# One whole-chunk subtraction on VectorE for the lower parts of U and V in a PEER kernel

## The chip, the cores and the metric

The kernel runs on one core of a Trainium2 chip. The metric is the device time of one execution in microseconds. The core has five engines with queues of their own, each of which runs its instructions in order: TensorE (PE in the profile, with its weight loads as PEld), VectorE (DVE), ScalarE (ACT), GpSimd (POOL) and SyncE (SP, which here only issues loads). Semaphores set the order between them.

## The reference, cut to what matters

Two layers run over 256 latent and 256 context tokens of width 1024: a gMLP mixer, then a state-space mixer, each followed by a PEER expert block. Of the context, only layer 0's result is needed. The change concerns the PEER blocks, whose 16384 experts (128 x 128 keys) each own a row of `u_tab` and of `v_tab`:

```python
q = (hb @ w_q).reshape(PEER_BLOCK, PEER_HEADS, 2, PEER_DHALF)
s = jnp.einsum("nhkd,hkmd->nhkm", q, sub_keys)
s_half, i_half = lax.top_k(s, PEER_TOPK)
...
ids = k1 * PEER_KEYS + k2
g = jax.nn.softmax(top_s, axis=-1)
ue = jnp.take(u_tab, ids, axis=0)
ve = jnp.take(v_tab, ids, axis=0)
act = jax.nn.gelu(jnp.einsum("nd,nhkd->nhk", hb, ue))
return jnp.einsum("nhk,nhkd->nd", g * act, ve)
```

## The kernel before

The kernel doesn't gather experts for most tokens. It computes every expert's activation for a block of tokens as a dense product, multiplies it with a matrix of gates that is zero where an expert wasn't chosen, and multiplies the result with the whole of V. In layer 0 this dense stage takes 384 tokens (`n`), and the remaining 128 context tokens go by gathered rows, with GpSimd issuing the indirect loads and VectorE doing the dot products (tile `gscr`, L611) and the weighted sums (tile `acc`, L624). In layer 1 all 256 tokens go through the dense stage.

The 16384 experts are taken in 128 chunks of 128. `front(k1)` (L707) loads a chunk of U (tile `ur`, 128 x 1024, 512 KB), multiplies it with the tokens and applies the gelu (`act`); `back(k1)` (L726) loads a chunk of V (`vr`), multiplies the activations with the gates (`w`, L741) and adds the product with V to sums that stay in PSUM.

Each float32 matrix product is made of three matmuls on a reduced-precision type: every operand is split into an upper part and a lower part (upper times upper, upper times lower, lower times upper; `mm3`, L305, for U, and L755 to L757 for V). `split` (L297) makes the upper part on ScalarE, a copy with a rounding (tiles `uh`, `vh`, `wh`), and the lower part by subtracting it from the source (`ul`, `vl`, `wl`, L303), on VectorE or on GpSimd: a counter `turn` and the two last arguments give the shares of the two.

Before the change each chunk of U and of V is split in two halves of 512 columns. U's halves go by `DV0 = (1, 2)` in layer 0 (one in three on VectorE) and by (1, 1) in layer 1; V's halves go by (1, 1). `UB = 5` halves of U and `VB = 4` halves of V are held. The raw chunks have buffers of their own: 3 for U (`UR`), 2 for V in layer 0 and 4 in layer 1 (`VR`).

The order of the work in `dense` (L692): first 62 chunks of U in layer 0 and 66 in layer 1 (`ahead` less 2), together with the routing and the making of the gates (`during`: VectorE makes `eq` and `o`, L676 and L680, TensorE multiplies them, L664 and L665). Results that aren't kept are written to memory. Then the loop over all 128 chunks of V runs, where for the remaining chunks `front(k1 + 8)` stands ahead of `back(k1)`. So the V loop begins with chunks of V alone and goes on with U and V in turn. In layer 0 the gathers are spread over this loop (`pump`). In the V loop TensorE's order is the program's; on the other engines a planner places each instruction by a simulated time. In layer 1's first stretch U's splits have a higher priority (`HP = (0, 1000)`).

Of the kernel before, what the change touches and what calls it, by code (L numbers as in the profile page):

```python
# [10 lines left out]
F32R = mybir.dt.float32r  # L11
# [7 lines left out]
P = 128  # L19
D = 1024  # L20
KB = D // P
# [4 lines left out]
KEYS = 128  # L26
# [20 lines left out]
TAIL0 = 0  # L47
WB = 2
KEEP0 = 8
UB = 5  # L50
VB = 4
ROWS = 4
EARLY0 = 8
MID0 = 18
AHEAD1 = 68
TAIL1 = 0
M = SEQ // L
HP = (0, 1000)
# [5 lines left out]
AR_ = (2, 4)  # L64
UR = (3, 3)
ACTB = (1, 2)
DV1 = (1, 1)
DV0 = (1, 2)
DVS = (DV0, (1, 1))
VV0 = (1, 1)  # L70
VV1 = (1, 1)
F1 = 4
PIN = 1
HA = 50
# [37 lines left out]
def tile_hybrid(ctx: ExitStack, tc: tile.TileContext, I, out, stop=None):  # L112
    nc = tc.nc
# [19 lines left out]
    def load(dst, src):  # L133
        return nc.sync.dma_start(dst, src)  # L134
# [162 lines left out]
    def split(hi, lo, src, dve=1, gps=1):  # L297


        turn[0] += 1  # L300
        nc.scalar.activation(hi, src, AF.Copy)  # L301
        e = nc.vector if turn[0] % (dve + gps) < dve else nc.gpsimd
        return e.tensor_tensor(lo, src, hi.bitcast(F32), op=OP.subtract)  # L303
# [386 lines left out]
    act_d = dr.tile([KEYS, P, NDENSE], F32, name="act_d")  # L690

    def dense(pd, back_pool, i, n, hh, hl, ahead, keep, abanks, vbanks, during, between, pump,  # L692
              dve=(0, 1), vdve=(1, 1), finish=None):


        nb = (n + P - 1) // P
        acts, gts = {}, {}
        kg, ng = 8, n // GT

        def gate_rows(blk, g0, g1):  # L700

            if blk not in gts:
                gts[blk] = pb.tile([P, ng, kg, GT], F32, name="Gr")
            load(gts[blk][:, g0:g1].rearrange("p g k n -> p g (k n)"),
                 gd[i][g0:g1, :, blk * kg:(blk + 1) * kg, :].rearrange("g p k n -> p g (k n)"))

        def front(k1, spill=False):  # L707
            u = pd.tile([P, KB, KEYS], F32, name="ur", bufs=UR[i])
            load(u, I[f"peer_ut{i}"][k1])
            pairs = []  # L710
            for q in range(2):
                uh = pd.tile([P, KB // 2, KEYS], F32R, name="uh", bufs=UB)
                ul = pd.tile([P, KB // 2, KEYS], F32R, name="ul", bufs=UB)
                with tc.high_priority(HP[i]) if k1 < ahead and HP[i] else ExitStack():
                    split(uh, ul, u[:, q * 4:q * 4 + 4], *(dve if k1 < ahead else DVS[i]))
                pairs += [((uh[:, b], ul[:, b]), (hh[:, 4 * q + b], hl[:, 4 * q + b])) for b in range(4)]
            pm = ps.tile([P, 512], F32, name=f"bk{abanks[k1 % len(abanks)]}")
            mm3(pm[:, :n], pairs)
            act = pd.tile([P, n], F32, name="act", bufs=keep + ACTB[i])
            nc.scalar.activation(act, pm[:, :n], AF.Gelu_apprx_tanh)  # L720
            if spill:
                eng[QS[2]].dma_start(act_d[k1, :, 0:n], act)
            else:
                acts[k1] = act

        def back(k1):  # L726
            blk, j = divmod(k1, kg)
            v = pb.tile([P, D], F32, name="vr", bufs=VR[i])
            load(v, I[f"peer_v{i}"][k1 * KEYS:(k1 + 1) * KEYS, :])
            if k1 in acts:  # L730
                act = acts.pop(k1)
            else:
                act = pb.tile([P, n], F32, name="actr", bufs=AR_[i])
                load(act, act_d[k1, :, 0:n])
            if k1 == 0:
                for g0 in range(0, ng, GB):
                    gate_rows(0, g0, min(ng, g0 + GB))
            if (blk + 1) * kg < KEYS:
                gate_rows(blk + 1, ng * j // kg, ng * (j + 1) // kg)
            w = pb.tile([P, n], F32, name="w", bufs=WB)  # L740
            nc.vector.tensor_tensor(w.rearrange("p (g n) -> p g n", n=GT),  # L741
                                    act.rearrange("p (g n) -> p g n", n=GT),
                                    gts[blk][:, :, j, :], op=OP.mult)
            wh = pb.tile([P, n], F32R, name="wh", bufs=WB + 1)
            wl = pb.tile([P, n], F32R, name="wl", bufs=WB + 1)
            ends["w"] = split(wh, wl, w, 1, 0).ins
            first, last = k1 == 0, k1 == KEYS - 1
            for q in range(2):
                vh = pb.tile([P, 512], F32R, name="vh", bufs=VB)
                vl = pb.tile([P, 512], F32R, name="vl", bufs=VB)  # L750
                split(vh, vl, v[:, q * 512:(q + 1) * 512], *vdve)
                for t in range(nb):
                    js = slice(t * P, min(n, (t + 1) * P))
                    o = vacc[t][q][0:js.stop - js.start]
                    nc.tensor.matmul(o, wh[:, js], vh, start=first, stop=False)  # L755
                    nc.tensor.matmul(o, wh[:, js], vl, start=False, stop=False)  # L756
                    nc.tensor.matmul(o, wl[:, js], vh, start=False, stop=last)  # L757

        for k1 in range(ahead - TF[i]):
            front(k1, k1 < ahead - keep)  # L760
            during(k1)
        between()
        with tc.issue_after(ends["gates"]):
            for k1 in range(ahead - TF[i], ahead):
                front(k1)
        order = tc.manual_schedule(engines={mybir.EngineType.PE})
        order.__enter__()
        pb = back_pool()
        vacc = [[ps.tile([P, 512], F32, name=f"bk{vbanks[2 * j + q]}") for q in range(2)] for j in range(nb)]
        total = 2 * KEYS - ahead  # L770
        done = 0
        for k1 in range(KEYS):
            if ahead <= k1 + keep < KEYS:
                front(k1 + keep)
                done += 1
            back(k1)
            done += 1
            pump(done / total)
        order.__exit__(None, None, None)
        if finish:  # L780
            return finish(vacc)
        use_banks(*abanks)
        for j in range(nb):
            m = min(n - j * P, P)
            acc = pb.tile([P, D], F32, name="vr", bufs=VR[i])
            for q in range(2):
                nc.scalar.copy(acc[0:m, q * 512:(q + 1) * 512], vacc[j][q][0:m])
            with urgent(HD):
                add_back(i, acc, j * P, m)
# [462 lines left out]
    def layer0():  # L1252
        n = NDENSE
# [52 lines left out]
        with pool("hx") as ph, pool("hold", side="right") as pk, ExitStack() as hold:  # L1306
            hh = ph.tile([P, KB, n], F32R, name="hxh")
            hl = ph.tile([P, KB, n], F32R, name="hxl")
# [10 lines left out]
            with pool("hc") as pc:  # L1319
# [4 lines left out]
                ahead = [next(weights)]  # L1324
# [39 lines left out]
            with pool("de0", 2) as pd, ExitStack() as rs:  # L1364
                early = EARLY0
                first = spread((work, 250, 0, 1), (gathers, early, 0, 1))
                rest = []

                def during(k):
                    first((k + 1) / (AHEAD0 - TAIL0 - TF[0]))  # L1370

                def between():
                    drain(work)
                    scr.close()
                    pa = rs.enter_context(pool("ada1", 2, side="right"))
                    cB = ada_silu(pa) if CB else None
                    phases = phase_units(pa)
                    ada = ada_rows(pa, LATE[NS:NQ], cB)
                    cut = (AHEAD0 - KEEP0) / (2 * KEYS - AHEAD0)
                    rest.append(spread((gathers, MID0, 0.0, cut), (gathers, 128 - early - MID0, cut, GEND), (phases, 53, *PW),  # L1380
                                       (ada, NQ - NS, *AW)))
                    use_banks(1)
                    rs.callback(lambda: [drain(gathers), drain(ada), drain(phases)])

                def back_work(t):
                    with tc.issue_after(ends["w"]) if PB_ <= t < PC_ else ExitStack():
                        rest[0](t)

                use_banks(2, 3, 4, 5, 6, 7)
                dense(pd, lambda: rs.enter_context(pool("db0", 2, side="right")), 0, n, hh, hl, AHEAD0, KEEP0, (0, 1), (2, 3, 4, 5, 6, 7),  # L1390
                      during, between, back_work, DV0, VV0)
            use_banks(*range(8))

    def layer1():
        n = SEQ
# [19 lines left out]
        with pool("hx1") as ph:  # L1415
            hh = ph.tile([P, KB, n], F32R, name="hxh")
            hl = ph.tile([P, KB, n], F32R, name="hxl")
# [7 lines left out]
            with pool("sc1", 2, side="right") as pw:  # L1425
                weights = score_weights(1, pw)
                ahead = [next(weights)]
# [8 lines left out]
            with pool("de1", 2) as pd, ExitStack() as rs:  # L1436
# [55 lines left out]
                        rest[0](t)  # L1492

                use_banks(2, 3, 4, 5, 6, 7)
                dense(pd, lambda: pd, 1, n, hh, hl, AHEAD1, 8, (0, 1), (4, 5, 6, 7), during, between, back_work1, DV1, VV1, finish)
                use_banks(*range(8))

    layer0()
# [66 lines left out]
```

## Time and profile before

| | us |
|---|---|
| median of 3 runs | 3009.76 (3003.44 to 3010.11) |
| the profiled execution | 2998.49 |
| its span | 2996.7 |
| TensorE busy | 2678.1 (89%) |
| VectorE busy | 2306.5 (77%) |
| ScalarE busy | 1307.0 (44%) |
| GpSimd busy | 1438.1 (48%) |

Shares over the whole span hide that the stretches differ. In the trace the dense stage of layer 0 lies from about 480 to 1830 us and that of layer 1 from about 2130 us to the end; between them, and before, other code runs that the change doesn't touch. A busy time is the time between an instruction's start and its end, whatever it did in it. "Idle before" is the time in which the engine had no instruction running just before one of a group, with what released it. In the names, `bk` is a PSUM bank, and `out<-in` tells what an instruction writes and reads.

### The profile page before, as it was taken

The numbers are of one execution on the slowest core, as the hardware profiler recorded it, in microseconds if no ns is written. First come the engines' busy times: TensorE is split into PE (matmuls) and PEld (weight loads), VectorE is DVE, ScalarE is ACT, GpSimd is POOL, SyncE is SP. The second block draws the span as 40 slices with busy tenths as digits, with TensorE's granted clock in tenths as the row PEclk, the third lists the DMA queues.
The fourth block names the chain that finished last, engine by engine and source line by source line (L and its number), as shares of the span: only waits on it lengthen the run. The fifth ranks groups of instructions, "written<-read, shape, count | busy, mean of one in ns | idle before, by whom it ended". The sixth has DMA issues, their size and how long they took to land.

```text
span 2996.7 us, 46002 instructions
## 1 busy us (share of the span) xinstructions
PE 2678.1 (89%) x16231; PEld 2375.2 (79%) x16231; DVE 2306.5 (77%) x3980; ACT 1307.0 (44%) x2412; POOL 1438.1 (48%) x1008
## 2 busy tenths in 40 slices
PE   6799899888878888999999987998788889999998
PEld 2599798888766666888888866798787888899997
DVE  7796879999977886999999986464899876644344
ACT  4553243354562233333333323334345665555554
POOL 2031134544634344788888871235454335544443
PEclk8899999999988999999999998999899999999999
DMA  8579743565658787898999987997366778866662
GB/s 276 156 241 338 258 152 123 179 223 191 228 201 268 266 295 255 310 319 311 326 305 316 312 271 253 332 342 204 113 197 232 284 266 297 275 213 216 204 208 104
DMA packets 414576, 738.89 MB, mean 247 GB/s; under 512 B 41604, under 2 KB 272260, under 8 KB 409224
## 3 DMA queue, kind: packets, MB, share of 16 engines
q1 hardware_dynamic: 310240, 507.84, 51.1%
q0 software_dynamic: 36864, 134.23, 13.1%
q10 hardware_dynamic: 67240, 93.88, 8.8%
q8 instruction: 127, 2.08, 0.3%
q14 instruction: 105, 0.86, 0.1%
HBM read 633.07 MB, written 102.77 MB: 246 GB/s over the span
## 4 chain that ended last, share of the span: by engine, by line
PE 31%; DMA 13%; DVE 11%; issue 7%; POOL 5%; ACT 1%; SPq 1%; DVEq 0%; ACTq 0%; POOLq 0%
PE bk L756 6%; PE bk L757 5%; PE bk L755 5%; PE bk L311 4%; PE bk L309 4%; PE bk L310 4%; DMA vr<-peer_v 3%; DMA row<-peer_v,ids 2%; POOL row L601 2%; DMA row<-peer_u,ids 2%; DVE ul L303 1%; POOL ul L303 1%; POOL vl L303 1%; PE bk L554 1%; SPq L134 1%
## 5 line engine op out<-in xcount | busy, mean ns | idle before, releaser
L311 PE MATMUL bk<-hxh,ul 128*128 128x384 f32 (+1 forms) x2048 | 649.5, 318 | 47.7 <-DVE ul L303 28.5
L309 PE MATMUL bk<-hxh,uh 128*128 128x384 f32 (+1 forms) x2048 | 649.6, 317 | 11.7 <-ACT uh L301 6.9
L310 PE MATMUL bk<-hxl,uh 128*128 128x384 f32 (+1 forms) x2048 | 643.8, 314 | 0.0
L303 POOL TENSOR_TENSOR ul<-ur,uh 128x512 fp32r<-128x512 f32 x299 | 447.1, 1501 | 301.9 <-ACT uh L301 268.7
L303 POOL TENSOR_TENSOR vl<-vr,vh 128x512 fp32r<-128x512 f32 x256 | 363.0, 1422 | 461.1 <-ACT vh L301 454.6
L756 PE MATMUL bk<-vl,wh 128*128 128x512 f32 x1280 | 517.8, 405 | 63.6 <-POOL vl L303 46.1
L755 PE MATMUL bk<-vh,wh 128*128 128x512 f32 x1280 | 511.5, 400 | 36.8 <-ACT wh L301 19.5
L301 ACT ACTIVATE vh<-vr 128x512 fp32r<-128x512 f32 x512 | 315.4, 623 | 519.2 <-DMA vr<-peer_v 375.9
L757 PE MATMUL bk<-vh,wl 128*128 128x512 f32 x1280 | 509.0, 398 | 0.0
L301 ACT ACTIVATE uh<-ur 128x512 fp32r<-128x512 f32 x512 | 315.5, 629 | 408.4 <-PE bk L310 226.6
L311 PEld LDWEIGHTS bk<-hxh,ul 128*128 128x128 f32 x2048 | 397.5, 194 | 55.5 <-DVE ul L303 33.8
L309 PEld LDWEIGHTS bk<-hxh,uh 128*128 128x128 f32 x2048 | 398.3, 194 | 18.9 <-ACT uh L301 7.9
L310 PEld LDWEIGHTS bk<-hxl,uh 128*128 128x128 f32 x2048 | 398.2, 194 | 5.0
L303 DVE TENSOR_TENSOR wl<-w,wh 128x384 fp32r<-128x384 f32 (+1 forms) x256 | 192.6, 753 | 242.0 <-ACT wh L301 241.4
L756 PEld LDWEIGHTS bk<-vl,wh 128*128 128x128 f32 x1280 | 246.8, 193 | 135.3 <-POOL vl L303 62.4
L755 PEld LDWEIGHTS bk<-vh,wh 128*128 128x128 f32 x1280 | 246.5, 193 | 92.0 <-ACT vh L301 22.7
L757 PEld LDWEIGHTS bk<-vh,wl 128*128 128x128 f32 x1280 | 247.1, 193 | 50.7 <-DVE wl L303 0.3
L303 DVE TENSOR_TENSOR vl<-vr,vh 128x512 fp32r<-128x512 f32 x256 | 205.2, 812 | 74.4 <-ACT vh L301 73.5
L624 DVE SCALAR_TENSOR_TENSOR acc<-row,wts,acc 128x1024 f32<-128x1024 f32 x127 | 208.3, 1640 | 21.2 <-DMA row<-peer_v,ids 20.1
L611 DVE SCALAR_TENSOR_TENSOR gscr<-row,hn 128x1024 f16<-128x1024 f32 x128 | 209.7, 1639 | 18.3 <-DMA row<-peer_u,ids 17.1
L303 DVE TENSOR_TENSOR ul<-ur,uh 128x512 fp32r<-128x512 f32 x213 | 188.7, 888 | 43.5 <-ACT uh L301 41.7
L223 DVE SCALAR_TENSOR_TENSOR adasv<-adatv,cB 128x1024 f16<-128x1024 f32 x112 | 157.3, 1405 | 61.0 <-DMA adatv<-ada_t 60.1
(325 smaller groups left out, 4966.1 us busy)
## 6 DMA issues: line engine op xcount, KB each, us to landing
ur<-peer_ut SPq DMA_DIRECT2D x256, 512.0 KB
vr<-peer_v SPq DMA_DIRECT2D x256, 512.0 KB
gd<-Gs ACTq DMA_DIRECT2D x40, 1024.0 KB
adatv<-ada_t SPq DMA_DIRECT2D x72, 512.0 KB
wqT<-peer_w_q SPq DMA_DIRECT2D x64, 512.0 KB
Gr<-gd SPq DMA_DIRECT2D x120, 192.0 KB
wp<-wpo ACTq DMA_DIRECT2D x32, 512.0 KB
wpi<-wp SPq DMA_DIRECT2D x16, 1024.0 KB
```

Of the source, the lines that this page charges most:

```text
L223: e.scalar_tensor_tensor(scr, w, 1.0, cB[:, t], op0=OP.mult, op1=OP.mult, accum_out=mod[:, i, f, t:t + 1])
L301: nc.scalar.activation(hi, src, AF.Copy)
L303: return e.tensor_tensor(lo, src, hi.bitcast(F32), op=OP.subtract)
L309: nc.tensor.matmul(o, ah, bh, start=(i == 0), stop=False)
L310: nc.tensor.matmul(o, ah, bl, start=False, stop=False)
L311: last = nc.tensor.matmul(o, al, bh, start=False, stop=(i == n - 1))
L601: tc.keep_in_program_order(nc.gpsimd.indirect_dma_start(out=r[:], out_offset=None, in_=I[f"peer_{table}{i}"], in_offset=bass.IndirectOffse ...
L611: nc.vector.scalar_tensor_tensor(scr, r, 1.0, hn, op0=OP.mult, op1=OP.mult, accum_out=dots[:, h, k:k + 1])
L624: nc.vector.scalar_tensor_tensor(acc, r, w, acc, op0=OP.mult, op1=OP.add)
L755: nc.tensor.matmul(o, wh[:, js], vh, start=first, stop=False)
L756: nc.tensor.matmul(o, wh[:, js], vl, start=False, stop=False)
L757: nc.tensor.matmul(o, wl[:, js], vh, start=False, stop=last)
```

## The change

The two halves become one operation each: for every chunk ScalarE makes the upper part of all 1024 columns in one instruction, and VectorE makes the lower part of all 1024 columns in one instruction. GpSimd makes none of them. Two whole chunks of U and two of V are buffered. The shares and the arguments that passed them are gone. The matmuls are the same in number, shape and order. `turn`, which also deals out the subtractions of other splits in the kernel, counts fewer splits.

```diff
-UB = 5
-VB = 4
+UB = 2
+VB = 2
...
-DV1 = (1, 1)
-DV0 = (1, 2)
-DVS = (DV0, (1, 1))
-VV0 = (1, 1)
-VV1 = (1, 1)
...
         def front(k1, spill=False):
...
-            pairs = []
-            for q in range(2):
-                uh = pd.tile([P, KB // 2, KEYS], F32R, name="uh", bufs=UB)
-                ul = pd.tile([P, KB // 2, KEYS], F32R, name="ul", bufs=UB)
-                with tc.high_priority(HP[i]) if k1 < ahead and HP[i] else ExitStack():
-                    split(uh, ul, u[:, q * 4:q * 4 + 4], *(dve if k1 < ahead else DVS[i]))
-                pairs += [((uh[:, b], ul[:, b]), (hh[:, 4 * q + b], hl[:, 4 * q + b])) for b in range(4)]
+            uh = pd.tile([P, KB, KEYS], F32R, name="uh", bufs=UB)
+            ul = pd.tile([P, KB, KEYS], F32R, name="ul", bufs=UB)
+            with tc.high_priority(HP[i]) if k1 < ahead and HP[i] else ExitStack():
+                split(uh, ul, u, 1, 0)
+            pairs = [((uh[:, b], ul[:, b]), (hh[:, b], hl[:, b])) for b in range(KB)]
...
+            vh = pb.tile([P, D], F32R, name="vh", bufs=VB)
+            vl = pb.tile([P, D], F32R, name="vl", bufs=VB)
+            split(vh, vl, v, 1, 0)
             for q in range(2):
-                vh = pb.tile([P, 512], F32R, name="vh", bufs=VB)
-                vl = pb.tile([P, 512], F32R, name="vl", bufs=VB)
-                split(vh, vl, v[:, q * 512:(q + 1) * 512], *vdve)
+                qs = slice(q * 512, (q + 1) * 512)
                 for t in range(nb):
                     js = slice(t * P, min(n, (t + 1) * P))
                     o = vacc[t][q][0:js.stop - js.start]
-                    nc.tensor.matmul(o, wh[:, js], vh, start=first, stop=False)
-                    nc.tensor.matmul(o, wh[:, js], vl, start=False, stop=False)
-                    nc.tensor.matmul(o, wl[:, js], vh, start=False, stop=last)
+                    nc.tensor.matmul(o, wh[:, js], vh[:, qs], start=first, stop=False)
+                    nc.tensor.matmul(o, wh[:, js], vl[:, qs], start=False, stop=False)
+                    nc.tensor.matmul(o, wl[:, js], vh[:, qs], start=False, stop=last)
```

## Rows read from the trace of the kernel before

**Rows 1.** Busy time by stretch, all engines: stretch, length, PE, PEld, DVE, ACT, POOL, granted clock, DMA.

```profile
480.00:890.00 410.00, 349.52 (x2290) 331.04 (x2291) 396.80 (x951) 208.40 (x308) 205.40 (x134) 0.91 0.56 198
890.00:1200.00 310.00, 259.94 (x1025) 199.57 (x1023) 234.88 (x389) 94.51 (x178) 131.00 (x105) 0.94 0.81 271
1200.00:1745.00 545.00, 518.41 (x2595) 465.31 (x2595) 508.33 (x508) 191.72 (x377) 448.46 (x324) 1.00 0.91 313
...
2130.00:2470.00 340.00, 288.57 (x2418) 275.62 (x2418) 300.78 (x600) 191.51 (x327) 159.79 (x96) 0.94 0.68 235
2470.00:2620.00 150.00, 150.00 (x664) 124.20 (x663) 93.32 (x167) 86.86 (x166) 74.51 (x55) 1.00 0.87 285
2620.00:2997.00 377.00, 363.45 (x2293) 329.56 (x2291) 159.32 (x278) 199.67 (x389) 165.13 (x125) 0.99 0.57 189
```

**Rows 2.** Timeline of DVE from 1499 us: start, duration (us), engine, line, operation, form.

```profile
1499.61 0.55 DVE L303 TENSOR_TENSOR wl<-w,wh 128x384 fp32r<-128x384 f32 x1
1500.19 2.05 DVE L741 TENSOR_TENSOR w<-act,Gr 128x384 f32<-128x384 f32 x1
...
1505.51 1.22 DVE L611 SCALAR_TENSOR_TENSOR gscr<-row,hn 128x1024 f16<-128x1024 f32 x1
```

**Rows 3.** Timeline of POOL, same stretch.

```profile
1500.51 1.31 POOL L303 TENSOR_TENSOR vl<-vr,vh 128x512 fp32r<-128x512 f32 x1
1501.97 1.09 POOL L601 DMA_INDIRECT row<-peer_u,ids  x1 [0.16 <-issue]
...
1505.75 1.81 POOL L601 DMA_INDIRECT row<-peer_u,ids  x1 [1.37 <-DVE gscr L611]
```

**Rows 4.** Groups of DVE, 2470 to 2620 us: count, busy us and mean ns, idle before.

```profile
L303 DVE TENSOR_TENSOR vl<-vr,vh 128x512 fp32r<-128x512 f32 x56 | 36.1, 685 | 0.3 <-ACT vh L301 0.3
```

**Rows 5.** By tile (gscr, acc, o): ns minimum, median, maximum; first and last start, us.

```profile
L611 DVE SCALAR_TENSOR_TENSOR gscr<-row,hn x128: 1197/1221/4989, 532.6 to 1716.7; 128x1024 f16<-128x1024 f32 x128
L624 DVE SCALAR_TENSOR_TENSOR acc<-row,wts,acc x127: 1268/1284/3960, 1049.2 to 1801.5; 128x1024 f32<-128x1024 f32 x127
...
L680 DVE TENSOR_TENSOR o<-eq,gt x160: 662/683/2887, 613.3 to 2432.0; 128x1024 f16<-128x1024 f16 x160
```

**Rows 6.** Groups of DVE, 1200 to 1745 us.

```profile
L611 DVE SCALAR_TENSOR_TENSOR gscr<-row,hn 128x1024 f16<-128x1024 f32 x92 | 157.5, 1712 | 17.3 <-DMA row<-peer_u,ids 16.2
L624 DVE SCALAR_TENSOR_TENSOR acc<-row,wts,acc 128x1024 f32<-128x1024 f32 x89 | 150.0, 1686 | 12.4 <-DMA row<-peer_v,ids 11.4
L303 DVE TENSOR_TENSOR wl<-w,wh 128x384 fp32r<-128x384 f32 x62 | 65.7, 1060 | 6.1 <-ACT wh L301 6.1
L303 DVE TENSOR_TENSOR vl<-vr,vh 128x512 fp32r<-128x512 f32 x63 | 63.7, 1013 | 0.0
...
L303 DVE TENSOR_TENSOR ul<-ur,uh 128x512 fp32r<-128x512 f32 x40 | 36.8, 920 | 0.0
```

**Rows 7.** Waits of PE, 1200 to 1745 us: waiter <- releaser: total us, times, longest.

```profile
PE bk L756 <- POOL vl L303: 24.8, 20, 2.8
```

**Rows 8.** Groups of DVE, 480 to 890 us.

```profile
L680 DVE TENSOR_TENSOR o<-eq,gt 128x1024 f16<-128x1024 f16 x96 | 78.6, 864 | 0.1
...
L303 DVE TENSOR_TENSOR ul<-ur,uh 128x512 fp32r<-128x512 f32 x43 | 41.3, 960 | 1.7 <-ACT uh L301 1.7
```

**Rows 9.** Waits of PE, 480 to 890 us.

```profile
PE bk L664 <- DVE o L680: 31.4, 19, 4.7
```

**Rows 10.** Waits of PE, 2110 to 2470 us.

```profile
PE bk L311 <- POOL ul L303: 16.6, 5, 9.4
PE bk L311 <- DVE ul L303: 16.2, 11, 4.3
```

**Rows 11.** Waits of SP, the queue that issues loads, 890 to 1200 us.

```profile
SPq L134 <- DVE vl L303: 73.5, 35, 8.7
```

**Rows 12.** Groups of ACT, 2470 to 2620 us.

```profile
L301 ACT ACTIVATE vh<-vr 128x512 fp32r<-128x512 f32 x111 | 69.3, 624 | 37.9 <-PE bk L757 19.5 <-issue 17.4 <-DMA vr<-peer_v 1.1
```

**Rows 13.** Groups of POOL, 480 to 890 us.

```profile
L303 POOL TENSOR_TENSOR ul<-ur,uh 128x512 fp32r<-128x512 f32 x87 | 141.8, 1639 | 157.3 <-ACT uh L301 139.5 <-PE bk L310 7.8 <-DVE si L474 5.4
```

More of the change, by code (lines that the diff above doesn't have):

```diff
@@ L692, in dense @@
     def dense(pd, back_pool, i, n, hh, hl, ahead, keep, abanks, vbanks, during, between, pump,
-              dve=(0, 1), vdve=(1, 1), finish=None):
+              finish=None):
         nb = (n + P - 1) // P
@@ L1390, in layer0 @@
                 dense(pd, lambda: rs.enter_context(pool("db0", 2, side="right")), 0, n, hh, hl, AHEAD0, KEEP0, (0, 1), (2, 3, 4, 5, 6, 7),
-                      during, between, back_work, DV0, VV0)
+                      during, between, back_work)
             use_banks(*range(8))
@@ L1494, in layer1 @@
                 use_banks(2, 3, 4, 5, 6, 7)
-                dense(pd, lambda: pd, 1, n, hh, hl, AHEAD1, 8, (0, 1), (4, 5, 6, 7), during, between, back_work1, DV1, VV1, finish)
+                dense(pd, lambda: pd, 1, n, hh, hl, AHEAD1, 8, (0, 1), (4, 5, 6, 7), during, between, back_work1, finish)
                 use_banks(*range(8))
```

## Prediction, made before the changed kernel was run

> **What bounds the kernel now.** I read the profile in this order: the busy times by stretch, then in each stretch which wait TensorE suffers, then the durations of VectorE's operations against their shortest forms, then GpSimd's queue. The table by stretch [rows 1] shows six stretches that the change touches, with different limits. In the first, 480 to 890 us (62 chunks of layer 0's U, with routing and gate work), VectorE is busy 396.8 of 410 us: it sets the pace. From 890 to 1200 us (V alone, 56 chunks) no engine is full; TensorE has 259.9 of 310. From 1200 to 1745 us (U and V together, 62 chunks, with the row gathers) TensorE has 518.4 of 545, VectorE 508.3, GpSimd 448.5 and the DMA engines 0.91: everything is nearly full. From 2130 to 2470 us (layer 1's U) VectorE has 300.8 of 340 and TensorE 288.6. From 2470 to 2620 us (layer 1's V) TensorE has 150.00 of 150, and from 2620 to the end it is as full but for the finish. A gain must come from the first four stretches; the last two can only lose.
>
> The second thing to see is why VectorE is so full. At 1500.19 us the product w, 384 columns, takes 2.05 us, while the operation before it, with as many columns, takes 0.55 [rows 2]. GpSimd's subtraction began at 1500.51 us and took 1.31 [rows 3], so it ended at 1501.82, and w ended 0.42 us later: VectorE stood still inside its instruction until GpSimd's was over. That time is counted as busy. So VectorE's share overstates its work by what GpSimd's subtractions take from it.
>
> **The change part by part.** *The subtractions.* The 512 halves of U and 512 of V, shared by VectorE and GpSimd, all go; 256 operations of 1024 columns for U and 256 for V come, all on VectorE. An undisturbed half takes 0.685 us [rows 4]. No subtraction of 1024 columns is in this trace; the nearest row is the dot product gscr, two inputs of 1024 columns, 1.221 us at the median [rows 5]. It is bounded from below by one half, 0.685, and from above by two, 1.37. I take 1.22, since the columns are the same.
>
> *VectorE from 1200 to 1745 us.* Out go ul with 36.8 us and vl with 63.7 [rows 6]. In come 62 chunks times two operations times 1.22, 151 us. And the standing still goes: gscr takes 1.712 on average against 1.221, over 92 operations 45 us; acc 1.686 against 1.284, over 89, 36 us; wl 1.060 against the 0.55 of [rows 2], over 62, 32 us [rows 2, 5, 6]. All GpSimd subtractions of this stretch are ul and vl, so I let all of it go: 508.3 - 100.5 + 151 - 113 = 446 us. VectorE does the whole of the work that two engines shared and has less to do than now. GpSimd keeps only the row gathers. TensorE waits 24.8 us for GpSimd's vl here [rows 7], because in GpSimd's queue a subtraction stands behind gathers that wait for VectorE to free a row buffer. That queue is what the change removes; vl then stands behind gscr and acc on VectorE instead, each at most 1.28 us when nothing stops it. The ceiling is TensorE's 545 - 518 = 27 us; the DMA share puts a floor at 0.91 x 545 = 496 us, so transfers allow it but become tight. I take 18 us of gain, bounds 27 and 0.
>
> A page of the Trainium skill bears on this: "SBUF — State Buffer", section "Who interferes with whom", infers that a two-input VectorE operation does not hinder the writing of descriptors for GpSimd's own transfers, so the gathers would be free of VectorE. The trace speaks against it: a gather takes 1.09 us at 1501.97, and 1.81 at 1505.75, beside a gscr that had begun at 1505.51 [rows 2, 3]. By the page, VectorE's added subtractions cost GpSimd nothing; by the rows up to 0.7 us for each of some 180 gathers, 130 us, on a queue that gives up every subtraction of this stretch. Either way the sum stays.
>
> *The first stretch.* Out go 43 VectorE halves, 41.3 us; in come 62 times 1.22, 76 us. From o, 0.864 against its 0.683, come back 17 us over 96 operations [rows 5, 8]. What the other groups lose (397 less 41 and 79 for ul and o, so 277 us) I bound from both sides: nothing, or o's share, 0.181 of 0.864, 58 us. VectorE's total: 397 - 41 + 76 - 17 - (0 to 58) = 357 to 415 us. GpSimd keeps its few products of the routing, which go on stopping VectorE, and many of the groups are short scans, so I take 27 of the 58: 388, a gain of 9 at VectorE's present 97%. TensorE waits here for gate operands, 31.4 us [rows 9], and these come sooner if VectorE is less held. I take 10 us, bounds 40 and -20.
>
> *Layer 1's U, 2130 to 2470 us.* Here half of the subtractions are on VectorE already: some 68 halves go, at the first stretch's 0.960 [rows 8] 65 us, and 68 operations of 1.22 us come, 83 us; 64 gate products at o's 0.181 give back 12 and the other groups as much again at least. VectorE ends near 295 of 340, so it isn't the limit, and nothing is lost. TensorE's waits for ul, 16.6 and 16.2 us [rows 10], are the ceiling, 33 us. The single waits for GpSimd's ul are long (9.4 us at most), which is a queue, not a price. I take 10, bounds 33 and -20.
>
> *V alone in layer 0, 890 to 1200 us.* The V buffer vr has two slots, and SyncE's next load waits for the last vl of the chunk before last: 73.5 us on VectorE's alone [rows 11]. Now the chain from landing is two ScalarE halves and the later of two subtractions; then it is one ScalarE operation, at most two of 0.624 [rows 12], and one of 1.22. With the 1.31 of GpSimd's that is 1.25 + 1.31 now against 1.25 + 1.22 then: even. What VectorE no longer loses inside w and wl shortens its queue. I take 5, bounds 20 and -15. The last layer-0 chunks after 1745 us I put at 2.
>
> *Layer 1's V, TensorE full.* U keeps two chunks (two and a half before), V two (in halves before). TensorE's 664 matmuls in 150 us [rows 1] are 55 chunks of 2.71 us. A V buffer comes free when a chunk's last matmul is done; then ScalarE, at most two halves' 1.25 us [rows 12], VectorE 1.22, and 11 of 12 matmuls, 2.5 us, must pass before it is free again: at most 5.0 us in a loop that has two chunks, 5.42 us, to do it. It fits with some 0.4 us to spare, so I cost it at nothing; that cover is thin, and it is a rival. With U and V together the loop has a U chunk more and is safe.
>
> Sum: 18 + 10 + 10 + 5 + 2 = 45 us. The profiled execution took 2998.5 us (span 2996.7), 11 below the median of 3009.8; against itself it would become 2953, and the median 2965. **I forecast 2965 us**, own range 2920 to 2998.
>
> **The rivals.** *VectorE inherits GpSimd's wait (slower).* GpSimd's ul stood 139.5 us waiting for ScalarE's uh in the first stretch, over 87 operations 1.6 us each [rows 13], and it cost nothing since nothing urgent was behind it. On VectorE the gates, the products and the gathers' arithmetic are queued behind a subtraction that waits, and TensorE waits for those. If VectorE, less held, runs ahead of ScalarE and inherits half of that, 0.8 us on each of the 130 U chunks of the two front stretches, it is 104 us: 3009.8 - 45 + 104 = 3069. It turns the gain into a loss from 0.35 us a chunk on. Against: VectorE's own 43 halves waited only 1.7 us for uh there [rows 8]. Chance 0.14.
>
> *The gain is hidden anyway (no change).* VectorE's total in the first stretch stays near 397, inside its bounds, and from 1200 us the transfers at 0.91 set the pace in TensorE's place; what remains is 5 to 10 us from layer 1. That gives about 3003. For it speaks that a single short wait is easily replaced by the next. Chance 0.14.
>
> *Two V chunks are too few in layer 1.* If VectorE has both 256-column operations of the next chunk ahead of the one in the loop above (0.42 us each, by the step from 0.55 at 384 columns to 0.685 at 512 [rows 2, 4]), and ScalarE its split of w (under the 0.62 of 512 columns), the loop takes 6.4 us in place of 5.42, 0.5 us a chunk, over 55 chunks 27 us: 2992. Chance 0.12.
>
> That the change does not do what it says is excluded: with shares of 1 and 0 every such subtraction goes to VectorE.
>
> **How the numbers follow.** The forecast has 0.60. A measurement here tells about 0.3%, 9 us, from no change. Faster by more: 0.60 and most of the third rival, 0.70. Within it: the second rival, 0.14. Slower: the first rival and a little of the bounds, 0.16. The range reaches from 2915, where most of the four ceilings is reached (27 + 40 + 33 + 20 is 120, of which I allow 95), to 3025, where the first rival has begun; beyond it some 0.12 is left above and 0.06 below.
>
> **What would show it.** Right: gscr at 1.22 and acc at 1.28 on average from 1200 us on, ul and vl of 1024 columns near 1.22, 256 each, no ul or vl on GpSimd; TensorE's wait for vl there under 10 us and the stretch near 527; the V stretch of layer 1 still at 150 with TensorE full. Wrong: VectorE's ul with over 20 us of idle time before it, released by ScalarE's uh, in the first stretch; TensorE waiting for vl after 2470 us; or a V-only stretch of layer 0 that grows because vr is loaded later.

## The result and the profile after

| | us |
|---|---|
| before, median (4 runs) | 3009.94 (3003.44 to 3011.40) |
| after, median (4 runs) | 2900.35 (2896.73 to 2910.35) |
| ratio | 0.964, 95% interval 0.9617 to 0.9663 |
| after, the profiled execution | 2899.56, span 2897.8 |

The change takes 110 us, 3.6%, off the median. The direction was forecast; the size was more than twice the 45 us of the forecast, and the time lies below the range's lower end of 2915. The two profiled executions differ by 99 us, since that of before was 11 us below its median. What follows accounts for those 99.

To compare stretches whose ends move, each is cut at the same two instructions in every kernel: the first split of U, then the first, the 57th, the 121st and the last split of w in layer 0, the first split of U in layer 1, and the first, the 61st and the 121st split of w in layer 1. The table gives the time between their starts on ScalarE, in us.

| stretch | before | after | difference | forecast |
|---|---|---|---|---|
| layer 0, U with routing and gates | 421.0 | 419.1 | -2 | -10 |
| layer 0, V alone (56 chunks) | 287.9 | 269.8 | -18 | -5 |
| layer 0, U and V (64 chunks) | 559.4 | 520.8 | -39 | -18 |
| layer 0, last chunks | 56.1 | 43.4 | -13 | -2 |
| the mixer of layer 1, up to its U | 349.8 | 345.5 | -4 | 0 |
| layer 1, U with routing and gates | 299.0 | 275.0 | -24 | -10 |
| layer 1, V alone (60 chunks) | 160.0 | 160.6 | +1 | 0 |
| layer 1, U and V, and the finish | 381.4 | 381.4 | 0 | 0 |

Busy time by stretch, after (stretch, length, PE, PEld, DVE, ACT, POOL, granted clock, DMA share, GB/s), which answers [rows 1]:

```profile
480.00:900.00 420.00, 346.15 (x2313) 326.34 (x2313) 394.19 (x976) 198.29 (x246) 79.04 (x51) 0.91 0.59 204
900.00:1170.00 270.00, 237.31 (x967) 189.18 (x968) 207.15 (x382) 83.00 (x111) 43.19 (x45) 0.94 0.88 296
1170.00:1690.00 520.00, 519.38 (x2639) 473.69 (x2638) 442.83 (x549) 184.97 (x258) 254.75 (x191) 1.00 0.96 339
...
2060.00:2370.00 310.00, 276.51 (x2371) 265.87 (x2371) 281.12 (x579) 176.37 (x242) 30.60 (x16) 0.95 0.74 255
2370.00:2520.00 150.00, 150.00 (x663) 124.22 (x662) 114.57 (x166) 75.87 (x111) 0.00 (x0) 1.00 0.88 285
2520.00:2898.00 378.00, 364.53 (x2298) 330.43 (x2296) 219.73 (x281) 175.21 (x266) 0.00 (x0) 0.99 0.58 190
```

The third row is the one to see. TensorE is busy 519.38 of 520 us; VectorE, which now does all the subtractions, 442.83 (508.33 of 545 before); GpSimd 254.75 (448.46). In the first row VectorE still has 394 of 420.

Groups of DVE from 1170 to 1690 us, after (count, busy us and mean ns, idle before and its releasers), which answer [rows 6]:

```profile
L619 DVE SCALAR_TENSOR_TENSOR acc<-row,wts,acc 128x1024 f32<-128x1024 f32 x100 | 128.1, 1281 | 10.6 <-DMA row<-peer_v,ids 9.9
L606 DVE SCALAR_TENSOR_TENSOR gscr<-row,hn 128x1024 f16<-128x1024 f32 x92 | 112.2, 1220 | 9.6 <-DMA row<-peer_u,ids 9.2
L298 DVE TENSOR_TENSOR vl<-vr,vh 128x1024 fp32r<-128x1024 f32 x64 | 78.1, 1220 | 5.9 <-ACT vh L296 5.8
L298 DVE TENSOR_TENSOR ul<-ur,uh 128x1024 fp32r<-128x1024 f32 x62 | 75.9, 1223 | 14.7 <-ACT uh L296 14.4
L298 DVE TENSOR_TENSOR wl<-w,wh 128x384 fp32r<-128x384 f32 x64 | 35.5, 555 | 35.9 <-ACT wh L296 35.9
L734 DVE TENSOR_TENSOR w<-act,Gr 128x384 f32<-128x384 f32 x64 | 35.4, 553 | 0.5
```

gscr went from 1.712 to 1.220 us and acc from 1.686 to 1.281, about the medians of [rows 5]; wl from 1.060 to 0.555. The product w, which [rows 6] leaves out, went from 0.883 to 0.553. Its row before:

```profile
L741 DVE TENSOR_TENSOR w<-act,Gr 128x384 f32<-128x384 f32 x61 | 53.9, 883 | 0.5
```

The new operations take 1.22. TensorE's only wait left in this stretch, against 24.8 us in [rows 7]:

```profile
PE bk L750 <- DVE vl L298: 0.6, 1, 0.6
```

In the first stretch TensorE's waits have changed their place rather than gone (480 to 900 us; [rows 9] had 31.4 us for the gate operand; the wait for ul was 12.3 before):

```profile
PE bk L306 <- DVE ul L298: 36.8, 14, 7.5
PE bk L659 <- DVE o L675: 18.1, 12, 6.2
```

And there two of VectorE's groups aren't at their short time, while the gate product o is (0.864 in [rows 8]); beside them stands GpSimd's product of the routing:

```profile
L298 DVE TENSOR_TENSOR ul<-ur,uh 128x1024 fp32r<-128x1024 f32 x66 | 88.3, 1337 | 10.1 <-ACT uh L296 10.1
L671 DVE TENSOR_TENSOR eq<-iot,kt 128x2048 f16<-128x2048 f16 x48 | 62.8, 1328 | 1.8 <-PE bk L660 1.7
L675 DVE TENSOR_TENSOR o<-eq,gt 128x1024 f16<-128x1024 f16 x96 | 60.8, 680 | 0.0
L506 POOL TENSOR_TENSOR oh<-oh,sf 128x1024 f32<-128x1024 f32 x14 | 42.3, 3022 | 275.0 <-DVE pi L500 222.8 <-DVE oh L504 52.2
```

### The profile page after: what moved, and what is told of

Its sections match the earlier page's. It is cut to its first block, busy times and chain, and to the rows that moved or that the text cites. A ratio compares the mean times of both kernels' runs of the same rounds, so it can differ in the third digit from the quotient of the medians.

```text
span 2897.8 us, 43990 instructions
## 1 busy us (share of the span) xinstructions
PE 2640.4 (91%) x16231; PEld 2361.3 (81%) x16231; DVE 2261.9 (78%) x4023; ACT 1231.5 (42%) x1900; POOL 634.0 (22%) x453
## 4 chain that ended last, share of the span: by engine, by line
PE 49%; DVE 8%; DMA 6%; issue 3%; POOL 2%; ACT 1%; SPq 0%; DVEq 0%; ACTq 0%; POOLq 0%
PE bk L750 8%; PE bk L751 8%; PE bk L749 8%; PE bk L306 7%; PE bk L304 7%; PE bk L305 7%; PE bk L549 2%; DMA vr<-peer_v 1%; DVE ul L298 1%; POOL row L596 1%; DVE vl L298 1%; PE bk L1148 1%; DMA row<-peer_v,ids 1%; DMA ur<-peer_ut 1%; DMA row<-peer_u,ids 1%
## 5 line engine op out<-in xcount | busy, mean ns | idle before, releaser
L304 PE MATMUL bk<-hxh,uh 128*128 128x384 f32 (+1 forms) x2048 | 645.1, 315 | 19.4 <-ACT act L713 12.3
L750 PE MATMUL bk<-vl,wh 128*128 128x512 f32 x1280 | 507.6, 397 | 25.1 <-DVE vl L298 25.1
L749 PE MATMUL bk<-vh,wh 128*128 128x512 f32 x1280 | 506.8, 396 | 20.0 <-ACT wh L296 10.1
L296 ACT ACTIVATE uh<-ur 128x1024 fp32r<-128x1024 f32 x256 | 271.4, 1061 | 551.1 <-PE bk L305 490.9
L298 DVE TENSOR_TENSOR ul<-ur,uh 128x1024 fp32r<-128x1024 f32 x256 | 328.3, 1282 | 130.7 <-ACT uh L296 130.2
L298 DVE TENSOR_TENSOR vl<-vr,vh 128x1024 fp32r<-128x1024 f32 x256 | 312.9, 1223 | 34.1 <-ACT vh L296 25.5
L296 ACT ACTIVATE wh<-w 128x384 fp32r<-128x384 f32 (+1 forms) x256 | 120.6, 471 | 509.0 <-PE bk L750 488.0
L749 PEld LDWEIGHTS bk<-vh,wh 128*128 128x128 f32 x1280 | 244.7, 191 | 70.8 <-ACT vh L296 12.4
L296 ACT ACTIVATE vh<-vr 128x1024 fp32r<-128x1024 f32 x256 | 267.7, 1046 | 56.5 <-DMA vr<-peer_v 44.5
L298 DVE TENSOR_TENSOR wl<-w,wh 128x384 fp32r<-128x384 f32 (+1 forms) x256 | 125.3, 490 | 165.0 <-ACT wh L296 164.5
L596 POOL DMA_INDIRECT row<-peer_v,ids x128 | 172.4, 1347 | 191.2 <-DVE acc L619 143.9
L596 POOL DMA_INDIRECT row<-peer_u,ids x128 | 163.1, 1274 | 210.6 <-DVE gscr L606 128.4
L619 DVE SCALAR_TENSOR_TENSOR acc<-row,wts,acc 128x1024 f32<-128x1024 f32 x127 | 162.6, 1281 | 16.3 <-DMA row<-peer_v,ids 15.5
```

The lines of the kernel that those rows point to most:

```text
L304: nc.tensor.matmul(o, ah, bh, start=(i == 0), stop=False)
L596: tc.keep_in_program_order(nc.gpsimd.indirect_dma_start(out=r[:], out_offset=None, in_=I[f"peer_{table}{i}"], in_offset=bass.IndirectOffse ...
L619: nc.vector.scalar_tensor_tensor(acc, r, w, acc, op0=OP.mult, op1=OP.add)
L749: nc.tensor.matmul(o, wh[:, js], vh[:, qs], start=first, stop=False)
L750: nc.tensor.matmul(o, wh[:, js], vl[:, qs], start=False, stop=False)
```

## The experiments

Three theories stood against each other at first. A: VectorE's two-input operations stand still while GpSimd subtracts, and taking that away is nearly all of the gain. B: half as many, twice as long instructions bring it. C: in GpSimd's queue subtractions stood behind gathers, and TensorE's data came late. The comparisons are with the kernel before, run on the same chip.

### The engine alone

```diff
-DV1 = (1, 1)
-DV0 = (1, 2)
-DVS = (DV0, (1, 1))
-VV0 = (1, 1)
-VV1 = (1, 1)
+DV1 = (1, 0)
+DV0 = (1, 0)
+DVS = (DV0, DV1)
+VV0 = (1, 0)
+VV1 = (1, 0)
```

> The kernel before with every ul and vl on VectorE, but still in halves of 512 columns and with 5 and 4 half buffers: the engine alone is changed. Theory A (VectorE stands still while GpSimd subtracts, and that is nearly all of the gain): about 2915 us, gscr back at 1.22 us, ul and vl at 0.68. Theory B (half as many, twice as long instructions bring the gain): 2980 to 3000, since 512 more instructions stay. Theory C (data stood in GpSimd's queue behind the gathers): about 2915, as A.

Measured: 2911.76 us against 3012.39, ratio 0.9661 (0.9628 to 0.9694). The interval holds the changed kernel's 0.964. So the choice of the engine is nearly all of the change: the changed kernel, run again on the same chip (2902.05 us, below), is some 10 us under it, a tenth of the gain. By stretch whole chunks are not nothing. With the engine alone the first stretch takes 427.8 us, longer than before (421.0) and than in the changed kernel (419.1), and layer 1's U 282.0 (299.0 and 275.0); V alone in layer 0 takes 263.3 us, less than the changed kernel's 269.8. U and V together take 518.3 us, 520.8 in the changed kernel. Theory B falls as the main cause.

### The form alone

```diff
-                split(uh, ul, u, 1, 0)
+                split(uh, ul, u, e=nc.gpsimd if k1 % (3 - i) else nc.vector)
...
-            split(vh, vl, v, 1, 0)
+            split(vh, vl, v, e=nc.gpsimd if k1 % 2 else nc.vector)
```

(`e` names the engine of the subtraction.)

> The changed kernel with whole chunks and two chunks buffered, but the subtractions dealt to both engines in the old shares (chunk by chunk: two of three U chunks of layer 0, every second U chunk of layer 1 and every second V chunk on GpSimd). The form alone is changed. Theory A: about 3000 us or above, since GpSimd's subtractions stop VectorE as before. Theory B: about 2930. Theory C: about 3010 or above, a chunk now stands whole behind the gathers.

Measured: 3044.99 us, ratio 1.0123 (1.0085 to 1.0161), so 1.2% above before. U and V together take 559.2 us, as before (559.4), with gscr at 1.731: nothing of the gain is there. What makes it slower is spread: the first stretch takes 432.6 us (421.0 before), and layer 1's U and its V alone take 483.7 us together (459.0 before, with the same 2846 matmuls). These two are taken together because 286 matmuls of U stand behind the first split of w in this kernel. GpSimd's subtraction of a whole chunk takes 2.39 us there, in a loop with two buffered chunks, and once U's matmuls are through, every second chunk of V takes 3.8 us, the others 2.7 as before. Group of POOL, and wait of PE, 2437 to 2654 us:

```profile
L298 POOL TENSOR_TENSOR vl<-vr,vh 128x1024 fp32r<-128x1024 f32 x28 | 67.0, 2392 | 106.3 <-ACT vh L296 106.3
```

```profile
PE bk L750 <- POOL vl L298: 18.0, 24, 0.8
```

The second row carries a lesson that the prediction lacked. The last 40 chunks of V alone (2524.3 to 2653.9 us) take 129.6 us, 108.8 before, so 20.8 are lost. TensorE's listed waits there are 14.9 us. The other 5.9 are counted as busy time: 114.66 us against 108.80 for the same 481 matmuls, at a granted clock of 1.00 in both. So a delay need not appear as idle time.

### GpSimd subtracting, or writing only, beside the changed kernel

Both kernels add work on GpSimd whose result nobody reads, in the places and numbers of the subtractions before; both hold the raw chunk until it is done. The first reads two inputs, the second only writes.

```diff
                 split(uh, ul, u, 1, 0)
+            for q in range(2):
+                if (2 * k1 + q) % (3 - i):
+                    nc.gpsimd.tensor_tensor(u[:, 0:4], u[:, 0:4], u[:, 4:8], op=OP.subtract)
...
             split(vh, vl, v, 1, 0)
+            nc.gpsimd.tensor_tensor(v[:, 0:512], v[:, 0:512], v[:, 512:1024], op=OP.subtract)
```

> The changed kernel, and GpSimd makes in addition as many subtractions of 512 columns as it did before (299 on the raw U, 256 on the raw V, after the split, results unused). TensorE waits for none of them. Theory A: VectorE's gscr goes back to about 1.7 us from 1200 us on, the time to 2970 to 3000. Theory B: 2900 to 2915. Theory C: 2905 to 2930, what the longer hold of the raw buffers costs, the same as e4.

In the second kernel each of these lines is `nc.gpsimd.memset(u, 0.0)` and `nc.gpsimd.memset(u[:, 0:3], 0.0)`, or the same with `v` and `v[:, 0:384]`.

> As e3, in the same places and with the same hold of the raw buffers, but GpSimd fills the raw chunk with zeros (1024 and 384 columns, together some 1.36 us, worked out from fills of 512 and 384 columns at 0.52 and 0.41) and reads nothing. Theory A, if reading is what stops VectorE: gscr stays at 1.22 us and the time is 2900 to 2920; if any GpSimd work stops it, as e3. Theory C: as e3, 2905 to 2930.

Measured: 3139.63 us (ratio 1.0431, 1.0399 to 1.0464) for the subtractions and 2968.26 us (0.9858, 0.983 to 0.9887) for the fills. DVE and POOL from 1200 to 1700 us, first with the subtractions, then with the fills:

```profile
L606 DVE SCALAR_TENSOR_TENSOR gscr<-row,hn 128x1024 f16<-128x1024 f32 x74 | 117.3, 1585 | 6.0 <-DMA row<-peer_u,ids 5.5
...
L298 DVE TENSOR_TENSOR ul<-ur,uh 128x1024 fp32r<-128x1024 f32 x44 | 76.3, 1734 | 0.0
...
L747 POOL TENSOR_TENSOR vr<-vr 128x512 f32<-128x512 f32 x58 | 96.9, 1671 | 54.5 <-DVE vl L298 42.3 <-issue 11.7
```

```profile
L606 DVE SCALAR_TENSOR_TENSOR gscr<-row,hn 128x1024 f16<-128x1024 f32 x91 | 111.3, 1223 | 39.4 <-DMA row<-peer_u,ids 38.7
L298 DVE TENSOR_TENSOR ul<-ur,uh 128x1024 fp32r<-128x1024 f32 x56 | 68.3, 1219 | 0.1
...
L711 POOL MEMSET ur<- 128x1024 f32 x74 | 71.7, 969 | 2.2 <-DVE ul L298 1.8
L712 POOL MEMSET ur<- 128x384 f32 x74 | 31.3, 422 | 3.5
```

GpSimd's fills, 0.969 + 0.422 = 1.39 us, leave gscr at 1.223 us and ul at 1.219; its subtractions, shorter when undisturbed (1.31 in [rows 3]), bring them to 1.585 and 1.734. So it is not GpSimd's being busy that stops VectorE, but its subtracting, which reads two inputs. From the first cut of U and V together to its last (596.6 us with the subtractions, 534.8 with the fills, 520.8 in the changed kernel) VectorE is busy 585.6 us beside the subtractions and 432.7 beside the fills, which is 1.06 us for each of GpSimd's 144 subtractions. Over the whole the two kernels differ by 171 us. This is more than the change gained, and the kernel with the subtractions is 140 us above the upper end of what was expected of it; that VectorE makes all the lower parts besides, and so has more to lose, is the likely reason and wasn't tested. This agrees with the Trainium skill, "SBUF — State Buffer", section "Who interferes with whom", which says that a two-input VectorE instruction contends with a GpSimd instruction that reads and not with one that only writes.

The fills still cost 68 us against the changed kernel, more than the 20 that were expected at most. In the row of gscr above VectorE had been idle 39.4 us for gathered rows (9.6 in the changed kernel): the gathers come later when GpSimd's queue holds other work, as theory C has it, and the raw buffers are held longer. Which of the two the 68 us come from isn't settled. Nor do the runs say how much of the gain is theory A's and how much C's. In U and V together TensorE's listed waits before were nearly all for GpSimd's vl (1191 to 1750 us), which stands in the queue of the gathers, and with U alone (below, 1203 to 1727 us), where V's subtractions still stand there, they are nearly gone; but that kernel relieves VectorE and the queue at once:

```profile
PE bk L756 <- POOL vl L303: 27.6, 22, 2.8
```

```profile
PE bk L754 <- POOL vl L303: 1.3, 1, 1.3
```

### V alone and U alone

The kernel before with the diff's part for V and `VB = 2`, or with its part for U and `UB = 2`.

> The kernel before with V's half of the change alone (whole chunks of V, on VectorE, two buffered; U as before). If the gain is what GpSimd's subtractions took from VectorE, stretch by stretch: V alone in layer 0 (288 us before) and the last chunks (56) gain as in the changed kernel, 18 and 13 us; U and V together gain about half of 39; the front stretches nothing. Sum about 50, 2960 us. If removing part of the subtractions is not enough, because the rest stops VectorE all the same: 2985 or above.

> The kernel before with U's half alone (whole chunks of U, on VectorE, two buffered; V as before). Layer 1's front stretch gains its 24 us, U and V together about half of 39, the first front stretch and the V stretches nothing: about 2965 us. If V's subtractions on GpSimd, still in the queue with the gathers, keep the stretch from 1200 us as it was: 2985.

Measured: V alone 2935.00 us (0.9736, 0.9703 to 0.9769), U alone 2946.74 (0.9788, 0.976 to 0.9817), both gaining more than expected. By stretch, as differences from before in us:

| stretch | V alone | U alone | both |
|---|---|---|---|
| layer 0, V alone | -21 | +10 | -18 |
| layer 0, U and V | -33 | -35 | -39 |
| layer 0, last chunks | -8 | -8 | -13 |
| layer 1, U with routing and gates | -1 | -27 | -24 |

Except in one stretch the gains add up to within 7 us. Why V alone in layer 0 is 10 us longer with U's half of the change isn't shown. With U and V together either half of the change gets nearly the whole, though gscr is then only a third of the way back with V alone and seven tenths with U alone. DVE from 1173 to 1699 us with V alone, and from 1203 to 1727 us with U alone:

```profile
L611 DVE SCALAR_TENSOR_TENSOR gscr<-row,hn 128x1024 f16<-128x1024 f32 x92 | 143.2, 1557 | 22.8 <-DMA row<-peer_u,ids 21.9
```

```profile
L611 DVE SCALAR_TENSOR_TENSOR gscr<-row,hn 128x1024 f16<-128x1024 f32 x94 | 127.7, 1359 | 20.1 <-DMA row<-peer_u,ids 19.7
```

The reason is the floor. In five kernels (changed, engine alone, and those with three buffers, with the priority and with oh, below) this stretch takes 518 to 521 us, with TensorE full; V alone reaches 526.0, U alone 524.4, with TensorE busy 522.6 and 522.1 us of it.

### The first stretch: buffers, place in the queue, or GpSimd's rest

Here the changed kernel gained 2 us. Three tries, each on the changed kernel: three buffers for U's upper part, a raised priority of U's splits in layer 0, and the routing's product on VectorE.

```diff
-            uh = pd.tile([P, KB, KEYS], F32R, name="uh", bufs=UB)
+            uh = pd.tile([P, KB, KEYS], F32R, name="uh", bufs=UB + 1)
```

> The changed kernel with three buffers for U's upper part and two for its lower part. In the first stretch of the changed kernel TensorE waits 36.8 us for ul (12.3 before) and ScalarE 178 us for a buffer of uh. If two buffered chunks are too few there, which ate the gain: the stretch gets 10 to 25 us shorter, 2875 to 2890. If VectorE's own load sets it (394 of 420 us busy): 2895 to 2905, no change.

```diff
-HP = (0, 1000)
+HP = (1000, 1000)
```

> The changed kernel with the same raised priority for U's splits in layer 0 that they have in layer 1, so that the planner puts ul ahead of the routing and gate work in VectorE's queue. If ul's place in the queue costs the first stretch its gain: 10 to 20 us shorter, 2880 to 2890; gate operands then wait. If VectorE's sum of work sets the stretch: within 5 us of 2900.

```diff
-                nc.gpsimd.tensor_tensor(oh, oh, sf[:, :, half, :].unsqueeze(2).to_broadcast(full), op=OP.mult)
+                nc.vector.tensor_tensor(oh, oh, sf[:, :, half, :].unsqueeze(2).to_broadcast(full), op=OP.mult)
```

> The changed kernel with the routing's product oh (24 operations of 1024 columns, 2.83 us each on GpSimd, 68 us in all) on VectorE too, about 1.22 us each, 29 us. If the same exchange holds in the front stretches (what GpSimd's remaining two-input products take from VectorE is more than they cost there): 5 to 20 us less, 2880 to 2895. If the first stretch is set by VectorE's own sum of work, at 394 of 420 us: 2900 to 2915, no gain or a loss of up to 17.

Measured: 2903.41 us with three buffers (0.965, 0.9617 to 0.9683) and 2909.27 with the priority (0.9662, 0.9635 to 0.9689), the first stretch 417.7 and 423.3 us: neither is the cause. With oh on VectorE 2873.26 us (0.9553, 0.9518 to 0.9589), 29 us below the unaltered changed kernel on the same chip, which was run beside it:

> The changed kernel itself, unaltered, on the same chip as e10 and e11, to compare them with: 2895 to 2912.

It measured 2902.05 us. The first stretch is now 405.4 us (419.6 beside it) and layer 1's 264.8 (274.8). DVE from 480 to 900 us with oh on VectorE, and TensorE's wait for ul there:

```profile
L298 DVE TENSOR_TENSOR ul<-ur,uh 128x1024 fp32r<-128x1024 f32 x66 | 80.2, 1215 | 10.5 <-ACT uh L296 10.4
...
L671 DVE TENSOR_TENSOR eq<-iot,kt 128x2048 f16<-128x2048 f16 x48 | 57.1, 1213 | 1.7 <-ACT kt L639 1.2 <-PE bk L660 0.5
...
L506 DVE TENSOR_TENSOR oh<-oh,sf 128x1024 f32<-128x1024 f32 x15 | 18.2, 1214 | 0.0
```

```profile
PE bk L306 <- DVE ul L298: 8.9, 6, 2.9
```

ul falls from 1.337 to 1.215 us, eq from 1.328 to 1.213, and TensorE waits 8.9 us for ul in place of 36.8. So the gain that was missing in the first stretch had stayed with GpSimd's few products, 3.0 us each. A part of it can come from a shorter chain of the routing and not from VectorE's standing still: VectorE had waited 5.3 us for GpSimd's oh in the changed kernel, and no longer does. The two aren't separated. Nor is every wait shorter: TensorE's wait for the routing's result k grew from 2.8 us to this:

```profile
PE bk L637 <- DVE k L507: 18.8, 2, 15.5
```

This is also the fastest kernel of the study.

### The other subtractions

As the last, and in addition:

```diff
-    def score_weights(i, pw, lo=(1, 2)):
+    def score_weights(i, pw, lo=(1, 0)):
...
-OW = (1, 2)
+OW = (1, 0)
```

> As e10, and the lower parts of the score weights (42 on GpSimd, 62 us) and of the state-space output weights (11, 29 us) on VectorE too. If taking GpSimd's subtractions away always pays: 2870 to 2890. If it pays only where TensorE waits behind VectorE or GpSimd, and these stretches are set otherwise: as e10 within 8 us.

Measured: 2875.13 us (0.956, 0.9526 to 0.9595), the same as without. Taking reads from GpSimd does not always pay. That these stretches are set by something else than VectorE, as the expectation has it, is likely and isn't shown.

## Why the prediction was wrong in size

**The mechanism was right.** VectorE stands still while GpSimd subtracts: shown by the two kernels with added work. The price of 1.22 us for 1024 columns was right (1.220 and 1.223 where nothing disturbs it). VectorE's total from 1200 us was forecast at 446 us, and is 442.83, but that is partly luck: over the same work (the two rows below) it fell by 77 us, from 521.85 to 444.83, where the forecast had 62. The time lost inside the product w, some 20 us, wasn't in its sum. Layer 1's V stretch was costed at nothing and is 160.6 against 160.0 us: the rival of too few V chunks did not happen, though the kernel that deals whole chunks to GpSimd, at 3.8 us for every second chunk, shows how thin the cover is. The rival in which VectorE inherits GpSimd's wait did not happen either: VectorE stood 10.1 us for uh in the first stretch, under the 20 that were named, and 18.3 in layer 1's U (12.4 before).

**U and V together, 18 forecast, 39 measured.** The ceiling of 27 us was mis-sized, and this is the largest part of the miss. It was taken as the stretch less TensorE's busy time. The same 2643 matmuls are busy 529.94 us before and 520.38 after:

```profile
1191.00:1750.00 559.00, 529.94 (x2643) 473.78 (x2643) 521.85 (x522) 195.08 (x385) 458.05 (x330) 1.00 0.90 310
```

```profile
1171.00:1692.00 521.00, 520.38 (x2643) 474.52 (x2642) 444.83 (x550) 185.02 (x259) 256.40 (x192) 1.00 0.95 339
```

The granted clock is 1.00 in both. So some 10 us of delay had been counted as busy, and the ceiling, worked out afterwards, was 559 - 520 = 39 us. Then two thirds of it were taken, out of care for the transfers; these went on at 339 GB/s with a share of 0.96 and did not set the pace. The whole ceiling was gained.

**V alone in layer 0, 5 forecast, 18 measured; the last chunks, 2 and 13.** The step that failed was the chain from landing to release, reckoned as even, 1.25 + 1.31 against 1.25 + 1.22. From the start of a chunk's first vh to the end of its last vl it measured 4.2 us on average before and 3.3 after. ScalarE's part went from 1.4 to 1.05 us, and the rest from 2.8 to 2.3: GpSimd's vl took 1.50 us on average in this stretch, not the 1.31 of one instance. That a subtraction waits less for its turn isn't seen, with 1.0 us between the end of its vh and its start in both, on average. The next loads came sooner, and ScalarE's wait for them, 890 to 1200 us before and 900 to 1170 after, went from the first of these rows to the second:

```profile
ACT vh L301 <- DMA vr<-peer_v: 130.9, 39, 8.4
```

```profile
ACT vh L296 <- DMA vr<-peer_v: 31.7, 17, 7.0
```

The run with V alone puts 21 us on V's own move there. The last chunks were given a number without being worked out; TensorE had waited 12.2 us for vl in them, 8.1 of it for GpSimd's, and waits 3.4 after.

**Layer 1's U, 10 forecast, 24 measured, and 4 in the mixer ahead of it.** The bounds held 33 us; the value was taken at a third without a row that said so. The wait for GpSimd's ul, 16.6 us, went whole, and that for VectorE's stayed, 16.2 us in [rows 10] against this, 2060 to 2370 us:

```profile
PE bk L306 <- DVE ul L298: 17.8, 11, 8.5
```

TensorE's busy time for the same matmuls fell by 6 us besides. The run with U alone has 27. The mixer's 4 us show nothing: it takes 343.0 to 352.5 us in the kernels that keep the subtractions on VectorE.

**The first stretch, 10 forecast, 2 measured.** VectorE's sum was put at 388 us, from 397; between the two cuts it went from 396.7 to 392.5. The step at fault is the term of 62 operations at 1.22 us, 76 us, for ul. There are 66 in the stretch, and at 1.337 us each, with GpSimd's oh still beside them, they take 88.3. The 17 us for o came (78.6 to 60.8), and the 27 us put down to the other groups were about right (some 30). Moving oh brings ul to its 1.215 and gives 14 us there.

So of the four stretches with a ceiling three came close to it, 39 of the 39 worked out afterwards, and 18 of 20 and 24 of 33 us of the bounds on record, where the forecast took a quarter to a half; the first got 2 of 40. The no-change rival, which rested on a new wait in the place of the old, fell with them.

## What to carry to other kernels

Before work is shared between VectorE and GpSimd, compare the mean time of VectorE's two-input operations with their shortest: if the mean is well above it while GpSimd reads, GpSimd's help is taken out of VectorE's time. Taking it away paid where TensorE waited behind that work; the one run that tried it elsewhere gained nothing. The ceiling of a stretch is its length less the time that its matmuls take where nothing disturbs them, not less TensorE's busy time and not the sum of its listed waits. Where TensorE is the next engine to be full, as with U and V together here, expect the ceiling and not a share of it; where VectorE stays the full one, as in the first stretch, the ceiling says nothing.

## What the runs showed of the hardware

A GpSimd fill of 1.39 us leaves a two-input VectorE operation at its 1.22 us, and a GpSimd subtraction of 1.31 us does not. GpSimd's subtraction of 1024 columns takes 2.39 us and VectorE's 1.22. The gathers did not become quicker when GpSimd had nothing else to do: 1.33 to 1.34 us each from 1170 us on in the changed kernel (1.37 before), longer than the 1.09 us of the single one in [rows 3]. Gathers are longer beside VectorE's two-input operations, as the prediction read it: with U and V together, those with such operations beside them for over nine tenths of their length take 1.22 us at the median before (148) and 1.67 after (121), those with less than a tenth 0.94 in both (10 and 14). What lengthens them wasn't tested.
